# Weight pages 2080 bytes apart and rows of h 4128 bytes apart in a hybrid attention and HGRN2 block

## The chip, the cores and the metric

The kernel runs on one core of one Trainium2 chip. The metric is the device time of one execution in microseconds. A core has five engines that run side by side: TensorE for matrix products (PE in the profile, with the loading of stationary operands shown apart as PEld), VectorE (DVE), ScalarE (ACT), GpSimd (POOL), and SyncE (SP), which here only starts transfers. Operands of TensorE lie in SBUF, the on-chip memory of 128 partitions; its results go to PSUM.

## The reference

The reference is one layer of a block with two branches over a sequence of 1024 tokens and 1024 channels.

```python
h = rms_norm(h_res, norm_w[layer])
z = jnp.einsum('bsd,dc->bsc', h, w_in[layer])          # 1024 x 1024 times 1024 x 12288
qkv_a, g_a, q_b, zf_fwd, zf_bwd, i_b, g_b, zgate_a, zgate_b = split(z)
# branch A: three groups of 8 heads, dilation 1, 4, 16: banded attention, merged by softmax weights
y_a = (o_a * silu(g_a)) @ w_proj_a
# branch B: HGRN2, forward and backward chunked scans over 8 heads of 128
y_b = (rms_norm(o_fwd + o_bwd, hg_norm_w) * silu(g_b)) @ w_proj_b
out = x + (sigmoid(zgate_a) * y_a + sigmoid(zgate_b) * y_b) @ w_out
```

All numbers are float32. Almost all of the arithmetic is in the product of h with w_in and in the three projections at the end.

## The kernel before

**Products in three parts.** A float32 operand x is kept as two tiles of the type fp32r: hi, which is x rounded to that type, and lo, which is x minus hi. A product of two such operands is three products: hi by hi, hi by lo, lo by hi. Every such product is a "wide" one here: a stationary operand of 128 by 128 numbers is loaded, and a moving operand of 128 partitions by 512 numbers (2048 bytes of each partition) runs through it. While one product runs, the stationary operand of the next one is loaded.

**h.** The normalised input, transposed, lies in two tiles hhi and hlo of 8 rows (one for each block of 128 channels) of 1024 tokens. They are made at the start and are read until the last product with w_in. They lie at the upper end of SBUF, in a pool of their own.

**Weights.** w_in, w_proj_a, w_proj_b and w_out come as 256 KB pages of 128 by 512 numbers. `Builder.feed` loads a page into one of four raw buffers; `Builder.split` has ScalarE write its hi and GpSimd (or VectorE, for pages with a scale) its lo. The hi and lo pages live in two rings of nine places each, "whi" and "wlo", set up in `setup_weights`; `free_to` gives a place back when the last product with the page has been issued.

**Three kinds of wide products over h** (`tok_group`, `T_group`, `run_quads`):

- `tok_group`: the tokens are stationary (`hhi[:, d, 128 tokens]`), the weight page moves. Its 128 tokens lie side by side in the first attention group and for the pages of i_b and g_b, 16 bytes apart in the second attention group, 32 bytes apart in the third.
- `T_group`: 128 columns of a weight page are stationary and 512 tokens of h move.
- `run_quads`: the gates by a Strassen scheme of seven products for eight, in part with sums of blocks of h, kept in tiles S0 to S3.

At the end, `evac_ya`, `evac_yb` and `evac_out` belong to three more rounds: the outputs of the branches are read back from DRAM through the ring "ld", split into tiles "sh" and "sl" (OA for branch A, OB for branch B), and move against stationary parts of weight pages; then the merged result, in tiles "mh" and "ml", is stationary and the pages of w_out move.

In `T_group`, a step over one block d of channels is

```python
return [(wh[:, c:c + 128], hhi[:, d, t]), (wh[:, c:c + 128], hlo[:, d, t]),
        (wl[:, c:c + 128], hhi[:, d, t])]
```

with the stationary operand first. c is 128 (d % 4), so that one page serves four blocks.

**Order.** The order of all instructions is written out by a planner in the kernel (`Plan`, `Builder.tick`, `Builder.burst`) before it runs. It keeps a time for every engine from fixed costs: a wide product has 512 / 2400 + 0.021 us in it. At set places between wide products it slips in small products (transposes, scores, the scan's products) whose operands should be there by its reckoning. `Builder.run_unit` issues a group of wide products and sets these places. The costs do not know where in SBUF a tile lies.

**Places.** Tiles of a pool lie one after another. As the kernel before is compiled, the nine whi pages begin at byte 25312 of a partition and lie 2048 bytes apart, the nine wlo pages follow at 43744, hhi begins at 163808 with rows 4096 bytes apart and hlo at 196576. All of these are 96 more than a multiple of 128, as are S0 to S3 and the sh and sl tiles of OB. The tiles of the pools that come behind the weights, with the mh and ml tiles, the sh and sl tiles of OA, and uhi and ulo (a first copy of h, without its row scale), are 32 more than a multiple of 128. In this document the remainder of an address by 128 is called its place.

Of the kernel before, what the change touches and what calls it, by code (L numbers as in the profile page):

```python
# [9 lines left out]
F32R = mybir.dt.float32r  # L10
# [8 lines left out]
S = 1024  # L19
# [190 lines left out]
class Builder:  # L210
# [89 lines left out]
    def setup_weights(self, items, pool, ring, raws):  # L300
        self.RING = ring
        self.wpages, self.windex, self.quads, self.steps = [], [], [], []
        n = 0
        for k, it in enumerate(items):
            if not isinstance(it, tuple):
                self.wpages.append(it)
                self.windex.append(n)
                n += 1
                continue
            m = len(self.quads)  # L310
            self.quads.append(it)
            more = k + 1 < len(items) and isinstance(items[k + 1], tuple)
            if k == 0 or not isinstance(items[k - 1], tuple):
                self.steps.append((n, m, "11"))
                n += 1
            for op in ("T1", "T2", "21", "T3", "+", "22", "T4"):
                if op != "+":
                    self.steps.append((n, m, op))
                    n += 1
                elif more:  # L320
                    self.steps.append((n, m + 1, "11"))
                    n += 1
        self.ops = n
        self.w = {}
        self.rawr = self.ring(pool, "raw", raws, [128, 512])
        self.hir = self.ring(pool, "whi", ring, [128, 512], F32R)
        self.lor = self.ring(pool, "wlo", ring, [128, 512], F32R)
        self.raws = []
        self.raw_next = 0
        self.split_next = 0  # L330
        self.freed = 0
        self.offered = None
        self.scales = {}
# [17 lines left out]
            self.offer(t, k)  # L351

    def split(self, raw):
        hi, lo = self.hir.get(), self.lor.get()
        scale = self.scales.get(self.split_next)
        if scale is None:
            self.p.act.activation(hi, raw, AF.Copy)
            self.p.pool.tensor_tensor(lo, raw, hi.bitcast(F32), op=OP.subtract)
        else:
            self.p.act.activation(hi, raw, AF.Copy, scale=scale)  # L360
            self.p.dve.scalar_tensor_tensor(lo, raw, scale, hi.bitcast(F32), op0=OP.mult, op1=OP.subtract)
        self.w[self.split_next] = (hi, lo)
        self.split_next += 1
# [10 lines left out]

    def free_to(self, n):
        for i in range(self.freed, n):
            hi, lo = self.w.pop(i)
            self.hir.done(hi)
            self.lor.done(lo)
        self.freed = max(self.freed, n)  # L380
# [184 lines left out]
def hybrid_block(ctx, tc, a, out):  # L565
    b = Builder(ctx, tc, a)
# [11 lines left out]
    hpool = hctx.enter_context(tc.tile_pool(name="hT", bufs=1, side="right"))  # L578
# [44 lines left out]
    a_.dma_start(ident, a["c_ident"])  # L623
    a_.dma_start(hwc, _dram(a["hg_norm_w"], 0, [[1, 128], [1, 1]]))

    hh_ = [hpool.tile([128, 8, S], F32R, name="hhi"), hpool.tile([128, 8, S], F32R, name="hlo")]
    hhi, hlo = hh_


# [1021 lines left out]
    ectx = {}  # L1651

    def end_start():
        bctx.close()
        ectx["ep"] = ep = ctx.enter_context(tc.tile_pool(name="end", bufs=1))
        ectx["ld"] = b.ring(ep, "ld", 6, [128, 512])
        for k in range(8):
            b.task("sp", [oaD], lambda k=k: split_load(OA, k % 4, k // 4, oaD[k % 4, k // 4],
                                                       lambda n: ep.tile([128, 512], F32R, tag="L", name=n, bufs=17)),
                   4, ectx["ld"].soon)  # L1660

    def split_load(to, j, half, src, new):
        t = ectx["ld"].get()
        s_.dma_start(t, src)
        b.task("act", [t], lambda: split_store(to, j, half, t, new), 4)
# [8 lines left out]
    n = 0  # L1674
    for j in range(TAIL, 8):
        for half in range(2):
            b.run_unit([T_group(pos, half, evac_sg(1, j, half), half == 1)])
            if not ectx and all(st.get("f", 0) == 2 for st in H.values()):
                end_start()
        pos += 2  # L1680
    b.drain()
    if not ectx:
        end_start()
        b.drain()
# [6 lines left out]
    ep = ectx["ep"]  # L1691
# [182 lines left out]
def _build(arrays):  # L1874
    import concourse.bacc as _bacc
    nc = _bacc.Bacc("TRN2", target_bir_lowering=False, num_devices=1)
    args = {n: nc.dram_tensor(f"in_{n}_dram", v.shape, mybir.dt.from_np(v.dtype), kind="ExternalInput").ap()
            for n, v in arrays.items()}
    out = nc.dram_tensor("out_0_dram", (S, D), F32, kind="ExternalOutput").ap()
    with tile.TileContext(nc) as tc:  # L1880
        hybrid_block(tc, args, out)
    return nc
# [9 lines left out]
```

## Time and profile before

| what | value |
|---|---|
| median of 3 runs | 1611.02 us (1607.05 to 1613.42) |
| the profiled execution: time, span | 1608.46 us, 1606.6 us |
| PE busy | 1569.1 us, 98% of the span, 8373 products |
| PEld busy | 1335.8 us, 83% |
| DVE, ACT, POOL busy | 845.3, 659.5, 468.0 us |
| DMA traffic | 148.31 MB |

The span is the time from the first to the last instruction of the profiled execution. A row of the groups of instructions reads: line, engine, operation, written tile <- read tiles, shapes, xcount | busy time in us, mean duration in ns of one | idle time before them and what ended it. For products, the tile named first after the arrow is the moving one and the second the stationary one. All instructions carry line 55, a helper that passes them on, so they are told apart by their tiles. A product's duration includes the time in which it drains, which overlaps the next product; how often products follow each other is read from their starts, or from the count in a stretch of time. In a table of stretches (windows), the columns are the stretch, its length, the busy time and count of each engine, the granted TensorE clock as a share of its full speed, the busy share of the DMA engines and GB/s.

### The profile page before, as it was taken

How to read it: one execution, taken by the hardware profiler on the slowest of the kernel's cores; microseconds unless marked ns; L12 is line 12 of the kernel's file. 1: busy time of each engine (PE TensorE's matmuls, PEld its weight loads, DVE VectorE, ACT ScalarE, POOL GpSimd, SP SyncE). 2: the span in 40 equal slices, each digit the busy share in tenths (PEclk: the TensorE clock that was granted, in tenths of full speed). 3: DMA queues.
4: the chain of work that ended last, by engine and by line, in shares of the span. 5: the costliest groups of instructions: out<-in, count | busy, mean ns of one | idle time of the engine just before them, and what ended most of it. 6: DMA issues, size and time to landing. Idle time of an engine off the chain costs nothing. (4 is left out here: it accounts for less than half of the span.)

```text
span 1606.6 us, 23188 instructions
## 1 busy us (share of the span) xinstructions
PE 1569.1 (98%) x8373; PEld 1335.8 (83%) x8373; DVE 845.3 (53%) x2216; ACT 659.5 (41%) x1434; POOL 468.0 (29%) x462
## 2 busy tenths in 40 slices
PE   8899999999999999999899999999999999999999
PEld 6688899999999987678788888888877878888887
DVE  5667632575136642336412207988889887543211
ACT  5533542434334363213334437655565554422110
POOL 3411202202022031228434434433344423003320
PEclk9999999999999999899999999999999999999999
DMA  6402203102022035473413251121221211842232
GB/s 215 139 22 98 70 18 112 50 33 67 21 63 66 16 103 138 125 219 112 144 66 115 83 166 40 53 93 40 54 86 47 94 39 65 293 140 92 88 119 89
DMA packets 110879, 148.31 MB, mean 92 GB/s; under 512 B 24625, under 2 KB 48300, under 8 KB 110764
## 3 DMA queue, kind: packets, MB, share of 16 engines
q1 hardware_dynamic: 103340, 146.38, 29.1%
q8 instruction: 66, 1.08, 0.3%
q10 hardware_dynamic: 7424, 0.45, 0.3%
q14 instruction: 49, 0.40, 0.1%
HBM read 110.77 MB, written 40.73 MB: 94 GB/s over the span
## 5 line engine op out<-in xcount | busy, mean ns | idle before, releaser
L55 POOL TENSOR_TENSOR wlo<-raw,whi 128x512 fp32r<-128x512 f32 x192 | 253.9, 1328 | 685.8 <-ACT whi L55 670.4
L55 PE MATMUL gp<-whi,hhi 128*128 128x512 f32 x792 | 328.5, 415 | 8.3 <-ACT stage L55 5.7
L55 PE MATMUL gp<-wlo,hhi 128*128 128x512 f32 x792 | 316.0, 399 | 1.4 <-POOL wlo L55 1.4
L55 PE MATMUL gp<-whi,hlo 128*128 128x512 f32 x792 | 316.1, 399 | 0.0
L55 PEld LDWEIGHTS gp<-whi,hhi 128*128 128x128 f32 x792 | 200.5, 253 | 36.8 <-issue 10.0
L55 PEld LDWEIGHTS gp<-wlo,hhi 128*128 128x128 f32 x792 | 201.4, 254 | 18.3 <-POOL wlo L55 2.6
L55 PEld LDWEIGHTS gp<-whi,hlo 128*128 128x128 f32 x792 | 200.9, 254 | 17.9 <-DVE hlo L55 1.0
L55 PE MATMUL gp<-hhi,whi 128*128 128x512 f32 x512 | 209.4, 409 | 0.0
L55 PE MATMUL gp<-hhi,wlo 128*128 128x512 f32 x512 | 200.9, 392 | 0.0
L55 PE MATMUL gp<-hlo,whi 128*128 128x512 f32 x512 | 200.0, 391 | 0.0
L55 ACT ACTIVATE whi<-raw 128x512 fp32r<-128x512 f32 x192 | 119.3, 626 | 140.9 <-PE gp L55 81.7
L55 PEld LDWEIGHTS gp<-hhi,wlo 128*128 128x128 f32 x512 | 96.2, 188 | 21.3
L55 PEld LDWEIGHTS gp<-hhi,whi 128*128 128x128 f32 x512 | 96.8, 189 | 18.8 <-issue 1.0
L55 PEld LDWEIGHTS gp<-hlo,whi 128*128 128x128 f32 x512 | 96.8, 189 | 17.2
L55 ACT ACTIVATE s<-s,neg 128x192 f32<-128x192 f32 (+2 forms) x192 | 83.9, 439 | 65.5 <-DVE neg L55 65.3
L55 DVE TENSOR_REDUCE ss<-sq 128x8 f32<-128x512 f32 x48 | 32.8, 684 | 146.7 <-ACT sq L55 146.7
L55 POOL TENSOR_TENSOR wlo<-qraw,whi 128x512 fp32r<-128x512 f32 x42 | 55.0, 1316 | 76.9 <-ACT whi L55 76.7
L55 PE MATMUL gp<-sh,whi 128*128 128x512 f32 x192 | 75.0, 391 | 0.0
L55 PE MATMUL gp<-sh,wlo 128*128 128x512 f32 x192 | 74.9, 390 | 0.0
L55 PE MATMUL gp<-sl,whi 128*128 128x512 f32 x192 | 74.6, 389 | 0.0
L55 ACT ACTIVATE sq<-gp 128x512 f32<-128x512 f32 x48 | 28.0, 592 | 111.8 <-PE gp L55 91.4
L55 ACT ACTIVATE stage<-gp 128x512 f32<-128x512 f32 x48 | 28.0, 594 | 111.5 <-PE gp L55 88.3
(225 smaller groups left out, 2787.9 us busy)
## 6 DMA issues: line engine op xcount, KB each, us to landing
raw<-in_w_in_dram SPq DMA_DIRECT2D x168, 256.0 KB
igD<-stage SPq DMA_DIRECT2D x32, 256.0 KB
ig<-igD SPq DMA_DIRECT2D x32, 256.0 KB
sgl<-sgD SPq DMA_DIRECT2D x32, 256.0 KB
oD<-os SPq DMA_DIRECT2D x48, 128.0 KB
og<-oD SPq DMA_DIRECT2D x24, 256.0 KB
qraw<-in_w_in_dram SPq DMA_DIRECT2D x24, 256.0 KB
sgD<-spare SPq DMA_DIRECT2D x24, 256.0 KB
```

The costliest lines, as they stand in the source:

```text
L55: got = f(*args, **kw)
```

## The change

Every page of the rings whi and wlo gets 520 numbers instead of 512, and every row of hhi and hlo 1032 instead of 1024. The numbers that are added are never written or read; all instructions keep their shapes. Pages then lie 2080 bytes apart and rows of h 4128 bytes apart, so that neighbours differ by 32 in their place. To make room, the ring "ld", through which the branch outputs are read back, has five buffers instead of six.

```diff
-        self.hir = self.ring(pool, "whi", ring, [128, 512], F32R)
-        self.lor = self.ring(pool, "wlo", ring, [128, 512], F32R)
+        self.hir = self.ring(pool, "whi", ring, [128, 520], F32R)
+        self.lor = self.ring(pool, "wlo", ring, [128, 520], F32R)
+        self.wt = {}
...
-        hi, lo = self.hir.get(), self.lor.get()
+        self.wt[self.split_next] = self.hir.get(), self.lor.get()
+        hi, lo = (t[:, 0:512] for t in self.wt[self.split_next])
...
-            hi, lo = self.w.pop(i)
+            self.w.pop(i)
+            hi, lo = self.wt.pop(i)
...
-    hh_ = [hpool.tile([128, 8, S], F32R, name="hhi"), hpool.tile([128, 8, S], F32R, name="hlo")]
+    hh_ = [hpool.tile([128, 8, S + 8], F32R, name=n)[:, :, 0:S] for n in ("hhi", "hlo")]
...
-        ectx["ld"] = b.ring(ep, "ld", 6, [128, 512])
+        ectx["ld"] = b.ring(ep, "ld", 5, [128, 512])
```

`self.wt` keeps the whole tiles beside the cut ones, since a ring knows its tiles by identity.

## The prediction

> **What bounds the kernel now.** I read the page first: which engine is busy, and whether its clock was held back.
>
> ```profile
> PE 1569.1 (98%) x8373; PEld 1335.8 (83%) x8373; DVE 845.3 (53%) x2216; ACT 659.5 (41%) x1434; POOL 468.0 (29%) x462
> PEclk9999999999999999899999999999999999999999
> ```
>
> TensorE is busy for 98% of the span at a full clock, and no other engine for more than 53%. What the change can do to the time is therefore what it does to the pace of products on TensorE. The groups of instructions, with shapes kept apart, tell how many wide products there are.
>
> ```profile
> L55 PE MATMUL gp<-whi,hhi 128*128 128x512 f32 x792 | 328.5, 415 | 8.3 <-ACT stage L55 5.7 <-ACT whi L55 1.5 <-ACT hhi L55 1.1
> L55 PE MATMUL gp<-hhi,whi 128*128 128x512 f32 x512 | 209.4, 409 | 0.0
> L55 PE MATMUL gp<-sh,whi 128*128 128x512 f32 x192 | 75.0, 391 | 0.0
> L55 PE MATMUL gp<-whi,mh 128*128 128x512 f32 x128 | 50.6, 396 | 0.0
> L55 PE MATMUL qA<-hhi,whi 128*128 128x512 f32 x48 | 18.7, 389 | 0.0
> L55 PE MATMUL qE<-S3h,whi 128*128 128x512 f32 x24 | 9.3, 389 | 0.0
> L55 PE MATMUL u<-whi,uhi 128*128 128x512 f32 x32 | 13.7, 428 | 0.0
> L55 PE MATMUL gp<-whi,uhi 128*128 128x512 f32 x8 | 3.2, 394 | 0.0
> ```
>
> Each row stands for three of its size, one for each part of the split product: 2376 from `tok_group` (moving whi, stationary h), 1536 from `T_group` (moving h), 576 with OA and OB, 384 with mh and ml, 144 and fifteen times 24 = 360 in `run_quads`, 96 and 24 with uhi and ulo. That is 5496 wide products. Now the pace: stretches that hold nothing on TensorE but wide products, in order of time `T_group` and `run_quads`; OA; OB; mh and ml.
>
> ```profile
> core 0: us, PE busy (x) PEld busy (x) DVE busy (x) ACT busy (x) POOL busy (x), PEclk, DMA share, GB/s
> 800.00:980.00 180.00, 180.00 (x796) 149.10 (x795) 41.31 (x63) 74.29 (x131) 78.73 (x71) 1.00 0.30 99
> 1383.00:1425.00 42.00, 42.00 (x185) 34.48 (x184) 26.25 (x41) 15.60 (x26) 0.00 (x0) 1.00 0.81 276
> 1430.00:1510.00 80.00, 80.00 (x355) 66.26 (x354) 24.80 (x36) 16.78 (x28) 28.32 (x22) 1.00 0.28 88
> 1520.00:1600.00 80.00, 80.00 (x345) 64.45 (x344) 9.68 (x14) 4.43 (x7) 9.06 (x7) 1.00 0.35 107
> ```
>
> A count holds two products that only reach into the stretch, so the products follow each other every 180 us / 794 = 226.7 ns, 42 / 183 = 229 ns, 80 / 353 = 226.6 ns and 80 / 343 = 233.2 ns. All four are the same kind of product at the same clock; PEld is far from full in each. What differs is the place: in the first and third all operands have place 96, in the second the moving sh and sl have 32 and the stationary pages 96, in the fourth the pages move at 96 and mh and ml stand at 32. The second also has heavy DMA traffic (0.81), the fourth hardly more than the third (0.35 and 0.28), so the fourth is the clean case: 6.6 ns for each product go with an unequal place. The order of time shows more, at the switch from OA (place 32) to OB (96).
>
> ```profile
> 1425.77 0.39 PE L55 MATMUL gp<-sh,wlo 128*128 128x512 f32 x1
> 1426.00 0.40 PE L55 MATMUL gp<-sh,whi 128*128 128x512 f32 x1
> 1426.23 0.39 PE L55 MATMUL gp<-sl,whi 128*128 128x512 f32 x1
> 1426.46 0.40 PE L55 MATMUL gp<-sh,wlo 128*128 128x512 f32 x1
> 1426.70 0.40 PE L55 MATMUL gp<-sh,whi 128*128 128x512 f32 x1
> ...
> 1428.32 0.39 PE L55 MATMUL gp<-sl,whi 128*128 128x512 f32 x1
> 1428.54 0.39 PE L55 MATMUL gp<-sh,wlo 128*128 128x512 f32 x1
> 1428.77 0.39 PE L55 MATMUL gp<-sh,whi 128*128 128x512 f32 x1
> 1428.99 0.39 PE L55 MATMUL gp<-sl,whi 128*128 128x512 f32 x1
> 1429.22 0.39 PE L55 MATMUL gp<-sh,wlo 128*128 128x512 f32 x1
> ```
>
> All places are equal from 1426.00 on, and still the first twelve products take 2.77 us, 231 ns each; only then does the pace settle at 226.6. So the quick pace is a settled one: moving reads and the next product's weight load fall into step, and after a switch of places this takes about a dozen products.
>
> **The change part by part.** Page k of a ring now starts 32 k further on than before, row d of hhi and hlo 32 d. The wlo ring begins 9 x 32 = 288 bytes later than now, so the wlo page of a pair stands 32 away from its whi page in place. In `T_group` the row of h changes every three products and within the three the stationary place goes whi, whi, wlo: no two steps in a row have the same distance of places. In `tok_group` the page and the row both step on, and wlo differs again. Nothing is issued more or less: same instructions, same shapes.
>
> A. Wide products that meet at place 96 today. Of `tok_group`'s 2376, the second and third attention groups (2 groups x 3 pages x 8 tiles x 24 = 1152) read h 16 or 32 bytes apart and stand under D; 1224 are left. With 1536 of `T_group`, 504 of `run_quads` and 384 with OB these are 3648. Their new pace has no row: no distance of 32 or 96 between wide operands occurs. From below: transposes load a stationary s (place 32) against a moving ident (place 64), an odd number of 32 bytes apart.
>
> ```profile
> 411.87 1.91 PE L55 MATMUL pT<-ident,s 128*128 128x128 f32 x16
> L55 PE MATMUL pT<-ident,s 128*128 128x128 f32 x312 | 39.9, 272 | 0.0
> ```
>
> Sixteen start within 1.91 - 0.27 = 1.64 us, 109.3 ns each for 128 columns. Wide products run at about half of that per column (226.7 / 512 against 109.3 / 128), so four at half the time, 218.6 ns, is the lower end for odd distances. From above: 233.2, the worst pace that lasts in a wide stretch. I take 231: it is what the unsettled products above took, it is the mean of the two lasting paces at unequal places (229 and 233.2 give 231.1), and the change never leaves the places alone for a dozen products. The stretches now settled lose 3648 x (231 - 226.7) = 15.7 us. Part of that is already paid: at some 80 breaks (an estimate: small products are slipped in at the edges of six groups in each of eight heads, and of the groups of the first attention group) ten products are unsettled today, 80 x 10 x 4.3 ns = 3.4 us. Net +12.3 us; at 229 it is 3648 x 2.3 - 3.4 = +5.0, at 233.2 it is 3648 x 6.5 - 3.4 = +20.3, and with half at 218.6 and half at 231 (mean 224.8) it is -6.9 - 3.4 = -10.3.
>
> B. The 384 products with mh and ml and the 120 with uhi and ulo stand at 32 today. The pools behind the weights move up by 2 x 288 = 576 bytes, 64 in place, so these come to 96, while the pages that they meet take all four: 504 x (231 - 233.2) = -1.1 us.
>
> C. The 192 with OA also come to 96: 192 x (231 - 229) = +0.4 us.
>
> D. The 1152 with h taken 16 or 32 bytes apart meet all places already within one load.
>
> ```profile
> 409.68 0.41 PE L55 MATMUL gp<-whi,hhi 128*128 128x512 f32 x1
> ...
> 411.63 0.41 PE L55 MATMUL gp<-whi,hlo 128*128 128x512 f32 x1
> ```
>
> Here are eight starts in 1.95 us, 244 ns each: slower than any wide product with adjacent columns, and the start of a row or page only turns the order in which places are met. I take nothing; a nanosecond either way is 1.2 us.
>
> E. The ring "ld" with five buffers for six. Its 24 loads serve OA and OB.
>
> ```profile
> L55 DVE TENSOR_TENSOR sl<-ld,sh x24: 681/684/1417, 1376.0 to 1413.1; 128x512 fp32r<-128x512 f32 x24
> L55 SPq DMA_DIRECT2D ld<-obD x16: 319/348/1772, 1386.1 to 1403.1; - x16
> ```
>
> OB is first needed at 1426.00; its last split starts at 1413.1. Sixteen loads through five buffers instead of six stretch 1386.1 to 1403.1 from 17 to 20.4 us and end some 3.4 us later: 9 us of cover are left, and with no cover it would cost the 3.4. For OA, the eighth tile could come late by one step of about 2 us (one buffer has to be read first), behind which the sgl loads of SP's queue would wait; taken as 0, at most 2.
>
> F. Small products (scores, transposes, scan): their tiles mostly move by 64 together, ident not. No row ties their pace to places; nothing taken. ACT and POOL, which write the pages, are busy 41% and 29%.
>
> Sum: 12.3 - 1.1 + 0.4 = +11.6 us. The profiled execution took 1608.46 us (span 1606.6 and 1.9 around it), so 1620.1; it lies 2.6 us under the median of the runs, 1611.02, so for a median 1622.6, taken as 1622.5. TensorE is the bound, so this lands in the time in full.
>
> **The rivals.**
>
> *No change.* If the reads settle at once for every distance, or the good and the bad distances cancel, the mean stays near 226.7: A gives 0, B 504 x -6.5 = -3.3, C -0.4. That is 1607 for a median. For it: a switch here is by one place, and the one at 1426.00 was by two. Against it: two unequal pairs were watched over hundreds of products and neither reached 226.7. The Trainium skill (TensorE: Matmul & The Clock Gate, Step-by-step: what each phase is for) says that TensorE has two independent SBUF read ports, so that loading the next weights takes no read bandwidth from the running product; by it no place would matter. The trace does not agree: 233.2 against 226.6 ns with the same shapes and clock.
>
> *Faster.* If an odd distance keeps the weight load out of the way of the moving reads as in the transposes, A gives -10.3, B 504 x (224.8 - 233.2) = -4.2, C 192 x (224.8 - 229) = -0.8, together -15.3: 1595.5. For it: half of the new pairs are odd, and 226.7 holds a surplus over 218.6 that something causes. Against it: the products with h 32 bytes apart touch odd distances all the time, at 244 ns, and a transpose moves its columns at half the rate, which leaves room. It decides as soon as odd pairs run below about 222 ns (with even ones at 231 the mean then is 226.5). The Trainium skill (TensorE: Matmul & The Clock Gate, Back-to-back issue gap) gives 512 / 2.4 + 2.5 = 215.8 ns for an undisturbed product; as an estimate from that page, 226.7 leaves 10.9 ns to be won where this forecast has a loss.
>
> *Worse than forecast.* If 233.2 becomes the rule everywhere, 1611 + 20.3 + 0.8 = 1632; this is the upper end of my first case, not a mechanism of its own.
>
> **How the numbers follow.** The forecast has 0.55, no change 0.23, faster 0.22. The first case alone reaches from 229 ns (5.0 - 2.1 = +2.9, 1614) to 233.2 (1632). What a measurement of this kernel can tell from no change is about 0.5%, 8 us: faster is below 1603, slower above 1619. Of the first case about 0.85 lies above 1619, which is 0.47 slower; its rest, 0.08, with 0.20 of no change and 0.01 of a mild faster case, is 0.29 the same; 0.21 of the faster case and 0.03 of no change are 0.24 faster. The range is 1599 to 1633: it leaves out the greater part of the faster case and what lies beyond 233 ns with a late tile.
>
> **What would show it.** Right: a stretch of OB or of the gates alone (`run_quads`) no longer shows 226.7 but about 231 ns per product, starts that differ by some 10 ns from one product to the next without settling; the stretch with mh and ml loses a little; counts of instructions, PE's waits and the end of the ld loads ahead of OB's start stay. Wrong: starts settled at 226.7 within three products (no change), or many starts under 222 ns (faster). If PE shows a new wait for sh or sl, E was mis-sized; if the products with h 16 or 32 bytes apart move by several ns, D was.

## The result and the profile after

The median of six runs is 1622.01 us (1621.13 to 1622.74) against 1609.03 us (1604.99 to 1613.42) for the kernel before in the runs beside it. The ratio is 1.0082 with a 95% interval of 1.0061 to 1.0102: slower, by about 13 us. The forecast was 1622.5. Executions of one kernel scatter with the granted clock (over 43 runs in the experiments the kernel before took 1613.05 us on average at a mean clock of 0.986, 1610.2 at 0.989 and 1603.9 at 0.995), and at 0.989 the kernel after took 1622.7, in one run, so the difference is not the clock's.

The profiled execution took 1621.13 us with a span of 1619.3 us, 12.7 us more than the 1606.6 of before. First the page of the kernel after: busy times with instruction counts, and the granted clock in 40 slices.

```profile
PE 1585.5 (98%) x8373; PEld 1337.7 (83%) x8373; DVE 845.1 (52%) x2216; ACT 661.2 (41%) x1434; POOL 467.7 (29%) x462
PEclk9999999999999999899999999999999999999999
```

The counts are those of before and the clock is as full. TensorE is busy 1585.5 - 1569.1 = 16.4 us longer (good to some 3 us, since single profiles of two kernels below that have the paces of before show 1571.3 and 1572.3), and idle 3.7 us less (1619.3 - 1585.5 = 33.8 us against 1606.6 - 1569.1 = 37.5). So no work was added and no wait: the products follow each other more slowly.

The table of stretches of the kernel after shows where (columns as in the prediction). In order of time: `run_quads` alone, OA, OB, mh and ml.

```profile
core 0: us, PE busy (x) PEld busy (x) DVE busy (x) ACT busy (x) POOL busy (x), PEclk, DMA share, GB/s
850.00:950.00 100.00, 100.00 (x432) 80.80 (x431) 20.44 (x31) 41.16 (x72) 46.28 (x37) 1.00 0.29 103
1390.00:1435.00 45.00, 45.00 (x195) 36.33 (x194) 27.05 (x43) 17.27 (x29) 1.29 (x1) 1.00 0.78 264
1440.00:1520.00 80.00, 80.00 (x346) 64.63 (x345) 24.12 (x35) 16.85 (x28) 26.80 (x21) 1.00 0.27 89
1530.00:1610.00 80.00, 80.00 (x347) 64.96 (x347) 10.00 (x16) 4.55 (x8) 10.39 (x8) 1.00 0.31 106
```

The same stretch in the kernel before, where `run_quads` ends at 943 us and `T_group` follows:

```profile
850.00:950.00 100.00, 100.00 (x442) 82.83 (x442) 19.99 (x32) 40.04 (x70) 47.10 (x41) 1.00 0.33 110
```

Without the two products that only reach in, that is 100 / 430 = 232.6 ns for a product of `run_quads` (before 100 / 440 = 227.3), 45 / 193 = 233.2 for OA (before 229), 80 / 344 = 232.6 for OB (before 226.6), 80 / 345 = 231.9 for mh and ml (before 233.2). One product more or less in a count is half a nanosecond in 100 us and over one in 45 us. All four stages now run at nearly one pace, and the two that had the quick one lost it. The order of time of the kernel after, within OB:

```profile
1440.83 0.39 PE L55 MATMUL gp<-sh,whi 128*128 128x512 f32 x1
1441.06 0.40 PE L55 MATMUL gp<-sl,whi 128*128 128x512 f32 x1
...
1442.91 0.40 PE L55 MATMUL gp<-sh,whi 128*128 128x512 f32 x1
1443.15 0.39 PE L55 MATMUL gp<-sl,whi 128*128 128x512 f32 x1
```

Ten products in 2.32 us, 232 ns each, 3.5 us after OB began; before, OB had come to 226.6 within 2.8 us.

### The profile page after: what moved, and what is told of

Same layout as the page of the kernel before. It is cut to its first block, busy times and chain, and to the rows that moved or that the text cites. A ratio compares the mean times of both kernels' runs of the same rounds, so it can differ in the third digit from the quotient of the medians.

```text
span 1619.3 us, 23185 instructions
## 1 busy us (share of the span) xinstructions
PE 1585.5 (98%) x8373; PEld 1337.7 (83%) x8373; DVE 845.1 (52%) x2216; ACT 661.2 (41%) x1434; POOL 467.7 (29%) x462
```

## The experiments

In the order in which they ran. Ratios are to the kernel before, measured beside each of them. Paces for a stage are means over the starts of its products: the time from one start to the next, where another wide product follows within 260 ns (longer gaps hold a wait, or lie in a stretch at a lower granted clock, such as 0.53 from 770 to 775 us in the kernel before). Each product is paired with the addresses of its operands as the kernel is compiled; where a row of a stretch says the same, it is shown. All of these rows are of the stretch from 850 to 950 us, `run_quads` (with the first products of the `T_group` behind it, in the kernels that get there sooner), unless their times say otherwise.

**Three constant shifts and the ring alone.** The first three move the whole rings whi and wlo by 32, 64 or 96 bytes, with pages still 2048 bytes apart and h where it was, so that every product of a stage meets one unequal place, the same each time. A second pad behind the weights brings the tiles there back to their place. The pads are 24 and 8 numbers of 4 bytes for the shift by 32, as shown, 16 and 16 for 64, 8 and 24 for 96. The fourth only takes a buffer from the ring ld.

```diff
+    stg.tile([128, 24], F32, tag="pads", name="pads", bufs=1)
     stage = b.ring(stg, "stage", 3, [128, 512])
...
+    wpool.tile([128, 8], F32, tag="padw", name="padw", bufs=1)
     b.setup_weights(items, wpool, RING, RAWS)
```

> All pages of whi and wlo moved together by 32 bytes (place 0), pitch 2048 as before, h at 96 as before: one constant, odd distance. Settling theory (the change costs because places never rest): the products of each stage settle after about a dozen, starts then repeat in a short pattern, no spread of 224 to 240 ns; the settled pace is unknown, between 224 and 234 ns. Rival distance theory (the loss is only the mean over the paces of the four distances, 231 to 232 ns): the lasting paces here and at 64 and 96 must average, with 226.7 for distance 0, to about 232, so at least one of them is near or above 233. Rival odd-is-better: under 222 ns and a time some 15 us below the kernel before.

Measured: 1625.48 us, 1.0084 (1.0068 to 1.0101).

```profile
850.00:950.00 100.00, 100.00 (x430) 80.52 (x429) 21.12 (x33) 41.43 (x72) 45.67 (x36) 1.00 0.31 102
```

100 / 428 = 233.6 ns; from the starts 233.3 in `run_quads` and OB, 233.1 in `T_group`, 233.3 in `tok_group` with adjacent tokens. Nothing changes from product to product here, and it never settles at the quick pace. It does settle: in OB the starts come 231 or 232 ns and 234 or 235 ns apart in turn, the short pattern that was expected.

> The same with 64 bytes (place 32 against 96). Settling theory: the lasting paces known from the kernel before return: 233.2 ns where the page stands and the other moves at 96 less 64 (as with mh and ml: pages at 32 against h at 96 in T_group, run_quads and OB, 2424 products, +6.5 ns each = +15.8 us), 229 ns where the page moves at 32 and h stands at 96 (as with OA: 1224 products, +2.3 = +2.8 us); OA and mh and ml now meet equal places: 226.7 (-3.7 us if the distance alone counts). Together about +12 to +15 us. Rival that only changes of place cost, not a resting distance: 0 to -4 us.

Measured: 1623.18 us, 1.0073 (1.0058 to 1.0088).

```profile
850.00:950.00 100.00, 100.00 (x431) 80.13 (x430) 20.43 (x31) 41.11 (x72) 45.83 (x36) 1.00 0.31 103
```

100 / 429 = 233.1 ns. `T_group`, `run_quads` and OB run at 233.3, but `tok_group`, which meets the same places with the roles exchanged (page moving, h stationary), at 229.2. Which operand lies ahead of the other matters. This was the first crack in the measure "places equal or not".

> The same with 96 bytes (place 64 against 96), the other odd distance. Settling theory: settled, repeating starts, pace unknown between 224 and 234 ns. Distance theory: the four lasting paces average about 232. Odd-is-better: about -15 us.

Measured: 1626.26 us, 1.009 (1.0075 to 1.0106).

```profile
850.00:950.00 100.00, 100.00 (x428) 80.42 (x427) 20.43 (x31) 40.92 (x72) 45.72 (x36) 1.00 0.30 101
```

100 / 426 = 234.7 ns; from the starts 234.2 to 234.4 in `run_quads` and OB, 233.3 in `tok_group`.

```diff
-        ectx["ld"] = b.ring(ep, "ld", 6, [128, 512])
+        ectx["ld"] = b.ring(ep, "ld", 5, [128, 512])
```

> The kernel before with the ring ld of five buffers alone. Both theories: no change of the pace anywhere; time within 0.2% of the kernel before, at most +2 us from a late eighth tile of OA; OB loads end up to 3.4 us later, still ahead of OB's start.

Measured: 1610.67 us, 0.9998 (0.9988 to 1.0007). The smaller ring costs nothing. Its loads for OB and its last split, with five buffers:

```profile
L55 SPq DMA_DIRECT2D ld<-obD x16: 319/320/483, 1387.5 to 1408.4; - x16
L55 DVE TENSOR_TENSOR sl<-ld,sh x24: 678/685/695, 1378.3 to 1415.2; 128x512 fp32r<-128x512 f32 x24
```

The loads take 20.9 us instead of 17, and the last split starts at 1415.2, 2.1 us later than before and 13 us ahead of OB, which begins at 1428.1.

**Equal places elsewhere, an equal unequal place, and pages 2176 bytes apart.** If only equality of places counts, then operands that all lie at place 0, or all at 64, must run as quickly as all at 96. The first two kernels move the pages up by 32 or 96 bytes, with the pads above, and h (with S and the tiles beside them) down by 96 or 32. The third moves the pages up by 32 and h down by 32, which leaves them 64 apart. The fourth puts the whi pages 2176 bytes apart, which is 17 times 128: all places stay 96.

```diff
     hh_ = [hpool.tile([128, 8, S], F32R, name="hhi"), hpool.tile([128, 8, S], F32R, name="hlo")]
+    hpool.tile([128, 24], F32, name="padh")
```

> Pages of whi and wlo and rows of h (with S0 to S3) all at place 0, pitches as before: equal places, as before, but another one. The runs at constant unequal places settled at 233.3 ns in nearly every stage, so what the change loses is the loss of the pairing of before, not the switching. Theory 'equal is enough': T_group, run_quads and tok_group run at 226.7 ns here, only OB (96 against 0) at 233.3: +2.5 us. Theory 'place 96 itself': 233 ns in these stages too, 1622 to 1626 us. In e_w64 the equal pair 32 and 32 (OA, mh and ml) ran at 232 to 233.3, which speaks for the second.

Measured: 1625.0 us, 1.0088 (1.0069 to 1.0107).

```profile
850.00:950.00 100.00, 100.00 (x430) 80.43 (x430) 20.81 (x32) 40.63 (x72) 46.56 (x36) 1.00 0.31 103
```

100 / 428 = 233.6 ns with all places equal. The expectation from equal places fell.

> All at place 64. 'Equal is enough': 226.7 ns, about +2.5 us (OB at 96 against 64: 234). 'Place 96 itself': 233 to 234 ns, 1622 to 1627 us. A third possibility, never seen yet: place 64, a multiple of 64, better than 226.7.

Measured: 1624.43 us, 1.0086 (1.0068 to 1.0103); `T_group`, `run_quads` and `tok_group` at 232.3 to 232.6 ns, hardly nearer to 226.7 than with place 0 (232.8 to 233.3).

> Pages at 0, h at 64: gives the two pairs that no run has had yet (page moving at 0 against h at 64 in tok_group, h moving at 64 against pages at 0 in T_group). 'Place 96 itself': about 233 ns in both; some pair under 226 would be a better layout.

Measured in one run: 1624.06 us, span 1622.2 us. `T_group` and `run_quads` 233.3, `tok_group` 229.2: the paces of the shift by 64 alone, although both operands lie elsewhere. So at these two distances the distance decides, and not where the operands lie.

```diff
-        self.hir = self.ring(pool, "whi", ring, [128, 512], F32R)
+        self.hir = self.ring(pool, "whi", ring, [128, 544], F32R)
```

(With the cut tiles `t[:, 0:512]` and five buffers in ld, as in the kernel after.)

> whi pages 2176 bytes apart (128 more), wlo pages 2048, ld of five: pitch changed, places all still 96. If the place within 128 bytes is what counts: 226.7 ns everywhere as before, time within 0.2%. If the distance is counted over 256 bytes or more, every second page would lose: about half of the 16 us.

Measured: 1621.22 us, 1.0066 (1.0046 to 1.0087).

```profile
850.00:950.00 100.00, 100.00 (x433) 81.39 (x432) 20.44 (x31) 41.35 (x72) 46.84 (x37) 1.00 0.31 102
```

100 / 431 = 232.0 ns, with every place at 96. The place as the prediction had it, an address by 128, is not the measure. When distances are taken by 256, the whi pages here lie 0 or 128 from h in turn, and the wlo pages, whose ring begins 9 x 128 bytes later, always 128; that is enough to lose the quick pace. Counted by 256, everything so far falls into line: the operands at equal places in the two kernels above were 128 apart, those of the kernel before 0 (whi, wlo, hhi, hlo, S and OB all lie 224 above a multiple of 256). The two pads of each kernel above that shifts the rings had moved the tiles behind the weights by 128, so in the expectations above the distances of OA, mh and ml, uhi and ulo are read by 128 and are not the ones that the products met; the table below has them by 256.

**The test of 256, and the two halves of the change.** One kernel moves the pages by 256 bytes; by the new measure nothing may change. One moves only the pools behind the weights by 192 bytes, so that OA, mh and ml, uhi and ulo also come to distance 0; it should gain. Two make the change by halves: only rows of h apart, or only pages apart, each with five buffers in ld. The edit of the second is shown; the first has 64 numbers there and 64 ahead of `setup_weights`; the halves are the lines of the change itself, with the other half left as before.

```diff
+    stg.tile([128, 48], F32, tag="pads", name="pads", bufs=1)
     stage = b.ring(stg, "stage", 3, [128, 512])
```

> Pages moved together by 256 bytes, the tiles behind them by 512. Read over 256 bytes instead of 128, all runs so far fit one table of the distance d = stationary less moving address: d = 0 rests at 226.7 ns, 192 at 229, 128 at about 233, 32, 64, 160 and 224 at 233.3, 96 at 234.3 (the equal places of e_all0 and e_all64 were 128 apart by this count). If 256 is the period, nothing changes here: 226.7 in T_group, run_quads, OB and tok_group, time within 0.2% of the kernel before. If it is 512, these stages go to about 233 and the time to about 1622.

Measured: 1611.33 us, 1.0008 (0.9997 to 1.0019).

```profile
850.00:950.00 100.00, 100.00 (x443) 82.81 (x442) 20.04 (x34) 40.04 (x70) 46.87 (x40) 1.00 0.32 109
```

100 / 441 = 226.8 ns: the pace of before, in every stage (OA 229.0, mh and ml 233.3). 32, 64 and 96 bytes cost 12 to 16 us, 256 nothing.

> The kernel before with the pools behind the weights 192 bytes further on, so that uhi and ulo, OA, mh and ml come to distance 0 mod 256 from the pages as well. By the table: mh and ml 233.3 to 226.7 (384 products, -2.5 us), uhi and ulo likewise (120, -0.8), OA 229 to 226.7 (192, -0.4): -3.7 us, 1607 us, 0.998 of the kernel before. If the slow pace at mh and ml has another cause than the distance, no change.

Measured: 1607.13 us, 0.9982 (0.9968 to 0.9996), the quickest kernel of this study and a little quicker than before. It was not quicker by its profile alone (TensorE busy 1569.6 us), which scatters by as much; the medians and the paces show it. So do runs with the same granted clock: at 0.989 its four lie between 1605.10 and 1607.28 us, 17 of the kernel before between 1608.64 and 1611.14. Its OA, OB, and mh and ml:

```profile
1385.00:1420.00 35.00, 35.00 (x156) 28.97 (x156) 24.60 (x38) 15.49 (x26) 0.55 (x1) 1.00 0.83 295
1425.00:1505.00 80.00, 80.00 (x355) 66.26 (x354) 24.84 (x37) 16.37 (x27) 24.46 (x19) 1.00 0.30 96
1515.00:1595.00 80.00, 80.00 (x355) 66.26 (x354) 11.06 (x16) 5.58 (x9) 11.67 (x10) 1.00 0.35 112
```

35 / 154 = 227.3, 80 / 353 = 226.6 and 226.6 ns (226.7 in all three from the starts). OA had 229 before under the same DMA load (0.81 there, 0.83 here), so that load was not what slowed it. The gain fits: 383 x 6.6 = 2.5, 192 x 2.3 = 0.4 and some 120 x 5.5 = 0.7 us make 3.6; measured 3.7 between the medians.

> Only the rows of h 4128 bytes apart, pages 2048, ld five: d changes with every row, all eight values in turn. Products with h lose as in the whole change (mean near 232, the mean of the eight resting paces), OB keeps 226.7, OA 229, mh and ml 233.3. The runs of 24 products with S tiles (distance 0, undisturbed) tell whether a dozen products are needed to settle: mean near 229 if so, 226.7 if each product has the pace of its own distance at once. PE busy +13 us, time +9 to +13 us.

Measured: 1619.27 us, 1.0062 (1.0042 to 1.0082). Products of h run at 232.0 (`tok_group`) and 232.4 (`T_group`, `run_quads`), OB stays at 226.7, mh and ml at 233.3. The products with S0 to S3 are the telling ones: their distance is always 0, and they come in runs of 12 or 24 behind products of h whose distance moves. The order of time of this kernel, a run of 24:

```profile
837.75 0.39 PE L55 MATMUL qE<-S0h,whi 128*128 128x512 f32 x1
837.98 0.40 PE L55 MATMUL qE<-S0l,whi 128*128 128x512 f32 x1
838.22 0.40 PE L55 MATMUL qE<-S0h,wlo 128*128 128x512 f32 x1
...
839.60 0.39 PE L55 MATMUL qE<-S0h,wlo 128*128 128x512 f32 x1
839.83 0.39 PE L55 MATMUL qE<-S0h,whi 128*128 128x512 f32 x1
840.06 0.39 PE L55 MATMUL qE<-S0l,whi 128*128 128x512 f32 x1
...
842.78 0.39 PE L55 MATMUL qA<-S1l,whi 128*128 128x512 f32 x1
843.01 0.39 PE L55 MATMUL qA<-S1h,wlo 128*128 128x512 f32 x1
```

The first nine take 839.83 - 837.75 = 2.08 us, 231 ns each; the next fourteen 3.18 us, 227 ns each. Over all 17 runs, the mean by position is 233, 231, 233, 229, 234, 231, 231, 231, 228, and 226.7 from the tenth product on. That is the settling which the prediction read from one switch of before, here after a different switch and in many runs.

> Only the pages 2080 bytes apart, rows of h 4096, ld five: all wide products with pages meet changing distances, mean near 232 in T_group, run_quads, tok_group and OB, mh and ml near 231 as in the whole change. Time as the whole change, 1620 to 1624 us: the two parts are not additive, since either alone already spreads the distances.

Measured: 1621.18 us, 1.0072 (1.0053 to 1.0092). `T_group`, S and OB 232.4 to 232.5, OA 232.7, `tok_group` and mh and ml 231.2 to 231.4. The halves give 0.62% and 0.72%, together 0.82%: not a sum, since most products lose their quick pace to either half.

**The pace by distance.** Distance is the address of the stationary operand minus that of the moving one, by 256, for stages where it stays the same from product to product. Means over the starts, as above.

| distance | ns per product | where seen |
|---|---|---|
| 0 | 226.7 | before: S, OB; pools behind the weights moved by 192: OA, mh and ml |
| 32 | 233.3 | pages +32: `run_quads`, OB |
| 64 | 233.3 | before: mh and ml; pages +64: `run_quads`, OB |
| 96 | 234.2 to 234.4 | pages +96: `run_quads`, OB, mh and ml; pages +32: OA |
| 128 | 232.3 to 233.3 | all at place 0, all at 64; pages +64: OA, mh and ml |
| 160 | 233.3 to 233.4 | pages +32: mh and ml; pages +96: `tok_group`, OA |
| 192 | 229.0 to 229.2 | before: OA; pages +64: `tok_group` |
| 224 | 233.3 | pages +32: `tok_group` |

In the three kernels that also move h, OA, OB, and mh and ml meet the same distances again as with pages +32 or +96 alone, and their paces lie within 0.1 ns of those.

## Why the prediction was right, and where it was not

**The mechanism.** Its two halves fared differently. That the quick pace is a settled one, lost at a switch and won back after about a dozen products, is shown (nine products in the runs with S). That it is equal places, taken by 128, which allow it, fell: four distances by 128 are eight by 256, and only one of the eight has 226.7. The kernel before happened to have that one in nearly all of its wide products, and the prediction took place 96 against 96 for the reason.

**A, the 3648 products at the quick pace.** Sign and size were right, the pace a little too low: 231 was taken. From the starts, before to after: `tok_group` with adjacent tokens 227.5 to 232.2 ns (1134 products), `T_group` and the h products of `run_quads` 228.2 to 232.5 (1556), S 226.7 to 232.5 (288), OB 226.8 to 232.4 (384). These are the 3362 which another wide product follows; their loss is 15.8 us, where 231 ns would have given 11.2 for them, and the forecast for all of A was 12.3. The credit for breaks already paid had the right size: the means before lie above 226.7 by 3.3 us in all, against 3.4.

Why 232.4 and not 231? The mean of the eight resting paces in the table is 232.0, so the sum cannot tell whether a product takes the pace of its own distance or never rests at all. The single products can. In the kernel after, take the 3527 products of `T_group`, `run_quads`, the pages of i_b and g_b, OA, OB, mh and ml that another wide product follows: their means by distance lie between 231.8 and 233.0, with 232.2 at distance 0 and 232.1 at 192. It is not the operand loaded meanwhile either: with the next product's stationary operand in the distance, the means lie between 231.5 and 232.8. They don't take a resting pace of their own. What the chip does inside in these nine products, and why 0 and 192 are better than their mirror images, stays open; no run here shows it.

**Odd distances.** The lower end, 218.6 ns from the transposes, was a wrong reading. 32, 96, 160 and 224 rest at 233.3 to 234.4, the slowest of all. The transposes, whose place also moved, stay at 109.2 ns each: their pace says nothing on wide products. The upper end, 233.2 as the worst pace that lasts, was exceeded by 96 (234.3); no stage of the kernel after rests there.

**B and C.** mh and ml went from 233.3 to 231.2 ns and uhi and ulo from 233.2 to 231.5, -1.0 us where -1.1 was forecast. OA went from 229.0 to 232.7, +0.7 where +0.4 was. Both terms now have their reason: B's products rested at distance 64, C's at 192.

**D, h 16 or 32 bytes apart.** Taken as 0. They went from 235.1 to 236.0 (16 bytes, 536 products) and from 244.9 to 245.5 (32 bytes, 534), +0.8 us, within the bound given.

**E, the ring.** The experiment with the ring alone gives 0.9998, so 0 was right. In the kernel after the last split came at 1424.2 and OB began at 1437.35:

```profile
L55 DVE TENSOR_TENSOR sl<-ld,sh x24: 683/687/693, 1386.5 to 1424.2; 128x512 fp32r<-128x512 f32 x24
```

**"TensorE is the bound, so this lands in the time in full."** Not quite. The terms above are 15.8 - 1.0 + 0.7 + 0.8 = 16.3 us, close to the 16.4 of busy time, but the span rose by 12.7 only. TensorE's waits in the kernel before and then in the kernel after (total us, times, longest):

```profile
PE gp L55 <- ACT stage L55: 5.7, 1, 5.7
PE U L55 <- ACT kT L55: 5.5, 4, 2.6
PE ss L55 <- DVE v L55: 4.4, 1, 4.4
```

```profile
PE U L55 <- ACT kT L55: 4.7, 3, 2.2
PE gp L55 <- ACT stage L55: 4.4, 1, 4.4
PE ss L55 <- DVE v L55: 3.5, 1, 3.5
```

The wait for stage is a single one near 770 us (in the kernel before it ends at 773.75); it lies between 4.3 and 5.9 us over all kernels here, slow or quick, and is taken as scatter. So is the wait for v, which is over by 31 us and lies between 3.8 and 4.4 us in all other kernels. The wait for kT is 5.5 to 5.8 us in the four kernels with the quick pace in `T_group`, `tok_group` and `run_quads` (before, five buffers, pages +256, pools +192) and 4.4 to 4.7 in all ten others. A likely reason, not tested, is that ScalarE keeps its pace, and a slower TensorE comes a little later to meet it. Without the wait for stage, the idle time of TensorE is 31.6 to 31.9 us in those four and 28.8 to 31.2 in the others. So a part of what the products lose comes back in waits: of the 3.7 us here, 1.3 are stage, 0.9 v, and at most 1.5 are left for it, 0.8 of them at kT.

The forecast of 11.6 us against 12.7 in the profiled span therefore holds two errors of opposite sign: 4.7 us too little for the products (3.5 of them in A, 0.8 in D), and 3.7 us of waits that were taken as unchanged. That 1622.5 came so near to 1622.01 is in part luck, the more so as the sum set out from a median of 1611.02 for the kernel before, which took 1609.03 in the runs beside the result.

**The rivals.** *No change* fell: no distance but 0 reaches 226.7, and the good and bad ones don't cancel. With the same products and clock and about the same DMA load (0.33 and 0.31), a shift of one operand by 32 bytes takes 226.7 to 233.3 ns. One rule went with this rival: the Trainium skill (TensorE: Matmul & The Clock Gate, Step-by-step: what each phase is for) gives TensorE two independent SBUF read ports. As far as the pace goes, that is not borne out here. Whether a read port, or something else in TensorE, makes the difference was not shown. *Faster* fell with the odd distances. The Trainium skill (TensorE: Matmul & The Clock Gate, Back-to-back issue gap) has 512 / 2.4 + 2.5 = 215.8 ns for a single product by itself. That was seen in no stretch. The best here is 226.7, at distance 0, so 10.9 ns stay unexplained.

## What to carry to other kernels

Where TensorE is the bound and each product loads a new stationary operand, read the pace from starts, stage by stage, and set it beside the addresses of both operands: here 128x512 fp32r products differ by 3% between stages for their distance by 256 bytes alone. In this kernel, pitches that are multiples of 256 bytes kept one distance, good or bad, for a whole loop; padding rows to spread the addresses, useful as it sounds, made this kernel 0.8% slower. One pad of 192 bytes ahead of the pools that had the wrong distance gave 0.2%.

## What the runs showed that was not expected

- The period is 256 bytes, twice what the prediction took for it: pages 256 bytes on run as before (1.0008), pages 2176 apart don't (1.0066), although 128 divides both.
- The sign matters: distance 192 rests at 229.0, distance 64 at 233.3.
- A distance that stays the same is not enough to settle at the quick pace. With operands 128 apart in the kernel with all at place 0, products keep 233.2 ns over the 772 of them between 800 and 980 us.
- The slow resting paces are settled too, as patterns of starts that repeat: in the kernel before 231 and then 235 or 236 ns in turn for mh and ml (distance 64), and a cycle of six from 225 to 232 ns for OA (192), where products at distance 0 come 226 or 227 ns apart.
- At distance 128 the pace is not settled by the distance alone: `run_quads` has 233.3 ns with all at place 0 and 232.3 to 232.4 with all at 64. Why is open.
- A product at distance 0 pays for its neighbours: 232.2 ns in the kernel after, 226.7 from the tenth in a row on that has that distance.
